# FFN hidden tiles in parts of 4, 4, 4, 4, 4, 2 in place of 4, 4, 4, 4, 6, with other look-ahead numbers

## Chip, core and metric

One NeuronCore of a Trainium2 chip runs the whole kernel as one launch. The metric is the device time of one execution in microseconds, the median of several runs.

## What is computed

A residual block on 512 tokens of width 1024 in float32: a SwiGLU FFN, a mixer stage (an HGRN2 recurrence and a Mamba-2 scan, merged by gates), a second SwiGLU FFN, a gated addition of per-layer embeddings, and a final RMSNorm. The change concerns the two FFNs only:

```python
D_MODEL, SEQ, D_FF = 1024, 512, 2816

def swiglu(x, w13, w2):
    gate, up = jnp.split(x @ w13, 2, axis=-1)
    return (jax.nn.silu(gate) * up) @ w2

h = h + 0.5 * swiglu(rms_norm(h, ffn1_norm[l]), ffn1_w13[l], ffn1_w2[l])
...                                        # mixer
h = h + 0.5 * swiglu(rms_norm(h, ffn2_norm[l]), ffn2_w13[l], ffn2_w2[l])
ple_gate = jax.nn.sigmoid(rms_norm(h, ple_norm[l]) @ w_ple_gate[l])
```

## The kernel before

**Numbers as pairs.** Every matmul operand is split into a high and a low part (`split`, L529 to L531: a cast on ScalarE, ACT, at L530 and a subtraction on VectorE, DVE, at L531). One product is three matmuls on TensorE, PE (`mm`, L518, L519, L520).

**The FFN.** The 2816 hidden columns are 22 tiles of 128, cut into the parts of `PARTS` (`ffn`, from L708). Hidden tiles are made two at a time (`gate_up`). Except for the first two tiles of all, a pair's gate and up columns are made by Strassen-Winograd: seven products instead of eight (`Seven`), each of 24 matmuls of 256 columns, one unit of the program each. Their weights come as one chunk of kind "w": five plain loads of 512 KB on the SP queue, two more that the POOL queue adds onto loaded pieces (L482), two sums on DVE (L503, L506), and seven pieces that are split.

**The down projection.** A part of four tiles keeps its hidden values in a `HiddenQ`: when its last pair is done (`put`), DVE makes four sums (`tsum`, L525, L527) and seven operands are split, 512 columns each. `down(k)` then is again seven Strassen products, one unit each, of 12 matmuls of 512 columns, with a "w" chunk of `w2` like that of `gate_up`. Each product is added to the tokens by two DVE operations (L780), 14 per part. The last part is another matter: its tiles lie in a `Hidden` (four splits of 256 columns per pair of tiles), and the function `last` does the plain product row by row: for each of the four token tiles t and two halves of the output, three matmuls of 512 columns per hidden tile, then one addition (L755). With six tiles these are 4 x 2 x 6 x 3 = 144 matmuls. Their weights are 6 chunks, one load and one split each.

**The order.** Units are emitted in a list. Part k's gate and up units stand merged with the down units of part k-1, after two units of their own:

```python
if k:
    U += x[:2] + _merge(x[2:], down(k - 1))
```

After the last part stand `n_end` (frees the normed input) and four units of `last`. Each ends with `done(t)`, which starts the norm of token tile t for the next stage (`norm_gen`, L565 to L569: a square on ACT, L567, two small POOL operations, a DVE multiplication, L569, then eight transposes on PE, L552, and four splits). After the first FFN the next units are the mixer's z projection, which takes one token tile after the other; after the second it is the gate projection of the embeddings. The list only fixes priorities and memory: a scheduler in the compiler orders each engine's instructions by its own simulated times, so work of later units can run ahead where it is ready.

**Look-ahead.** Before each unit, `run` (L443) loads and splits the pieces of later units, and loads raw ones further on. The six numbers of `AHEAD_FFN` are: how far ahead to split (near and far) and to load, in steps of 512 values per partition, and how many empty blocks of 4 KB per partition must be left by the near, far and raw ones (`room`). A piece of FFN weights counts 2 steps. All memory is one arena of 50 blocks; a load onto a block waits until the block's last reader is done.

Of the kernel before, what the change touches and what calls it, by code (L numbers as in the profile page):

```python
# [39 lines left out]
AHEAD = (4, 8, 10, 4, 8, 8)  # L40
AHEAD_SSD = (4, 9, 12, 4, 6, 8)
AHEAD_GATES = (2, 6, 8, 4, 8, 8)
AHEAD_FFN = (6, 10, 16, 1, 3, 3)

AGE = 130
PACK, PACK_MIX, PACK_GATES = 4, 2.5, 3
# [5 lines left out]

GATES_FIRST, LATE = 12, 2

PARTS = (4, 4, 4, 4, 6)

_INS = (
    "x", "p", "ffn1_norm", "ffn1_w13", "ffn1_w2", "mix_norm", "w_in", "conv_w", "conv_b", "dt_bias",
# [5 lines left out]
def _cols(c):  # L64
    return slice(c * P, (c + 1) * P)
# [281 lines left out]
class Block:  # L347
# [359 lines left out]
    def ffn(self, h, n, w13, w2, done, then=None):  # L707

        U = self.units
        start = len(U)  # L710
        f0s = [sum(PARTS[:k]) for k in range(len(PARTS) + 1)]
        N = len(PARTS)
        hid = [HiddenQ(self) for _ in PARTS[:-1]] + [Hidden(self, PARTS[-1])]
        v = self.nc.vector
# [19 lines left out]
        def gate_up(k, i):  # L734
            f = f0s[k] + i
            if f == 0:
                ch = [Chunk(w13, 0, KD, off, 2 * P, "c") for off in (0, FF)]
                return [Unit([c.halves[j] for j in range(2) for c in ch], first)]
            ch = Chunk(w13, 0, KD, f * P, 4 * P, "w", FF + f * P)
            q = Seven(self, n, lambda o, A, put=hid[k].put: gated(o, A, put, i))  # L740
            return [Unit([next(x for x in ch.halves if x.j == PRODUCTS[p][0])], lambda wt, p=p: q.product(wt, p, FFN_PACE))
                    for p in ORDER]
# [10 lines left out]
        def add(bank, t, ds):  # L753
            hd = h[0][t][:, ds * 512:ds * 512 + 512]
            v.scalar_tensor_tensor(hd, bank, 0.5, hd, ALU.mult, ALU.add)  # L755
            self.frb(bank)
# [30 lines left out]
        def last(*wt, t):  # L787

            q = len(wt) // 2
            for ds in range(2):  # L790
                bank = self.bank()
                for x in range(PARTS[-1]):
                    wh, wl = wt[ds * q + x // 2]
                    self.mm(bank, hid[-1].at(x, _cols(t)), (wh[:, x % 2], wl[:, x % 2]), x == 0, x == PARTS[-1] - 1)
                add(bank, t, ds)
# [13 lines left out]

        for k, size in enumerate(PARTS):  # L810
            x = [u for i in range(0, size, 2) for u in gate_up(k, i)]
# [9 lines left out]
        for u in U[start:]:  # L821
            u.ahead = AHEAD_FFN

# [808 lines left out]
```

## Time and profile before

| | us |
|---|---|
| median of 3 runs | 1578.18 (1575.81 to 1579.27) |
| the profiled execution | 1577.02 |
| its span in the trace | 1575.3 |
| PE busy in the span | 1537.3 |
| DVE busy in the span | 1081.1 |

The profiled execution has 1.7 us outside its span, and lies 1.2 us below the median. The first FFN fills the span from about 47 to 378 us, the second from about 1177 to 1523 us; the mixer lies between, the embedding gate behind. Matmuls overlap in the records (one of 512 columns is shown with 0.4 us, though they start 0.22 us apart), so a matmul's price is read from how many fit into a stretch without idle time.

### The profile page before, as it was taken

How to read it: one execution, taken by the hardware profiler on the slowest of the kernel's cores; microseconds unless marked ns; L12 is line 12 of the kernel's file. 1: busy time of each engine (PE TensorE's matmuls, PEld its weight loads, DVE VectorE, ACT ScalarE, POOL GpSimd, SP SyncE). 2: the span in 40 equal slices, each digit the busy share in tenths (PEclk: the TensorE clock that was granted, in tenths of full speed). 3: DMA queues.
4: the chain of work that ended last, by engine and by line, in shares of the span. 5: the costliest groups of instructions: out<-in, count | busy, mean ns of one | idle time of the engine just before them, and what ended most of it. 6: DMA issues, size and time to landing. Idle time of an engine off the chain costs nothing.

```text
span 1575.3 us, 22345 instructions
## 1 busy us (share of the span) xinstructions
PE 1537.3 (98%) x8894; PEld 1339.3 (85%) x8894; DVE 1081.1 (69%) x1379; ACT 754.5 (48%) x1093; POOL 173.3 (11%) x230
## 2 busy tenths in 40 slices
PE   8999999999998999999999999999999999999997
PEld 7989999988886887878888788888889999999986
DVE  7789888775568675867646654434348987897853
ACT  6555554554456445452454455433136654545542
POOL 2101101000012010110012011100002011001000
PEclk9999999999999999999999999999999999999999
DMA  9967867565233254364431522342239768676521
GB/s 298 213 160 189 214 147 192 123 208 161 67 95 108 88 167 141 120 182 141 121 100 61 174 69 72 107 134 94 94 90 236 171 175 206 148 193 148 200 68 54
DMA packets 216012, 225.52 MB, mean 143 GB/s; under 512 B 8148, under 2 KB 171748, under 8 KB 215908
## 3 DMA queue, kind: packets, MB, share of 16 engines
q1 hardware_dynamic: 190436, 194.73, 39.9%
q0 software_dynamic: 25472, 29.36, 11.7%
q8 instruction: 70, 1.15, 0.3%
q14 instruction: 34, 0.28, 0.0%
HBM read 209.31 MB, written 14.75 MB: 142 GB/s over the span
## 4 chain that ended last, share of the span: by engine, by line
PE 45%; DMA 5%; DVE 3%; ACT 2%; issue 1%; POOL 1%; DVEq 0%; POOLq 0%; ACTq 0%
PE bank L518 14%; PE bank L519 14%; PE bank L520 14%; DMA blk<-in_ffn_w_dram 4%; DVE blk L531 2%; ACT blk L530 1%; DMA blk<-in_w_in_dram 1%; PE bank L1336 0%; PE bank L1363 0%; PE bank L1331 0%; PE bank L1333 0%; PE bank L1351 0%; PE bank L1110 0%; PE bank L552 0%; PE bank L1365 0%
## 5 line engine op out<-in xcount | busy, mean ns | idle before, releaser
L518 PE MATMUL bank<-blk,blk 128*128 128x512 f32 (+1 forms) x2616 | 900.8, 346 | 17.4 <-ACT blk L530 7.7
L519 PE MATMUL bank<-blk,blk 128*128 128x512 f32 (+1 forms) x2616 | 898.2, 344 | 0.2 <-DVE blk L531 0.2
L520 PE MATMUL bank<-blk,blk 128*128 128x512 f32 (+1 forms) x2616 | 894.0, 344 | 2.5 <-DVE blk L531 2.5
L531 DVE TENSOR_TENSOR blk<-blk,blk 128x1024 fp32r<-128x1024 f32 (+2 forms) x477 | 493.7, 1059 | 206.0 <-ACT blk L530 166.4
L530 ACT CAST blk<-blk 128x1024 fp32r<-128x1024 f32 (+2 forms) x477 | 422.4, 920 | 388.2 <-DMA blk<-in_w_in_dram 79.2
L518 PEld LDWEIGHTS bank<-blk,blk 128*128 128x128 f32 x2616 | 498.0, 191 | 74.6 <-ACT blk L530 9.4
L520 PEld LDWEIGHTS bank<-blk,blk 128*128 128x128 f32 x2616 | 497.1, 191 | 56.0 <-DVE blk L531 2.9
L519 PEld LDWEIGHTS bank<-blk,blk 128*128 128x128 f32 x2616 | 498.8, 191 | 52.9 <-issue 1.0
L482 POOL DMA_DIRECT2D blk<-in_ffn_w_dram x56 | 70.8, 1265 | 484.0 <-DMA blk<-in_ffn_w_dram 384.6
L561 POOL TENSOR_SCALAR small<-small 128x1 f32<-128x1 f32 (+1 forms) x40 | 13.4, 334 | 615.2 <-ACT blk L567 293.6
L780 DVE SCALAR_TENSOR_TENSOR blk<-bank,blk 128x512 f32<-128x512 f32 x112 | 74.7, 682 | 2.3 <-PE bank L520 2.2
L883 ACT COPY blk<-bank 128x512 f32<-128x512 f32 x80 | 46.2, 581 | 45.5 <-PE bank L520 45.4
L995 DVE SCALAR_TENSOR_TENSOR blk<-bank,small,blk 128x511 f32<-128x511 f32 (+2 forms) x72 | 53.6, 744 | 15.1 <-ACT blk L993 14.4
L503 DVE TENSOR_TENSOR blk<-blk,blk 128x1024 f32<-128x1024 f32 x28 | 34.2, 1220 | 37.7 <-DMA blk<-in_ffn_w_dram 37.7
L748 ACT ACTIVATE blk<-blk 128x512 f32<-128x512 f32 x40 | 25.3, 632 | 61.7 <-DVE blk L893 45.8
L1110 PEld LDWEIGHTS bank<-blk,blk 128*128 128x128 f32 x256 | 40.9, 192 | 11.5 <-issue 6.0
L531 DVE TENSOR_TENSOR blk<-bank,blk 128x256 fp32r<-128x256 f32 x68 | 27.0, 418 | 18.8 <-ACT blk L530 18.7
L1110 PE MATMUL bank<-blk,blk 128*128 128x64 f32 x256 | 37.2, 259 | 1.6 <-DVE blk L531 1.6
L993 ACT ACTIVATE blk<-bank,small 128x512 f32<-128x512 f32 x24 | 18.6, 775 | 37.7 <-PE bank L520 37.7
L530 ACT CAST blk<-bank 128x256 fp32r<-128x256 f32 x68 | 23.4, 373 | 25.3 <-PE bank L552 25.1
L1071 DVE TENSOR_TENSOR blk<-blk,blk 128x1024 f32<-128x1024 f32 x16 | 19.6, 1222 | 21.6 <-POOL blk L1069 21.6
L506 DVE TENSOR_TENSOR blk<-blk,blk 128x1024 f32<-128x1024 f32 x28 | 34.1, 1216 | 0.0
(206 smaller groups left out, 1021.0 us busy)
## 6 DMA issues: line engine op xcount, KB each, us to landing
blk<-in_ffn_w_dram SPq DMA_DIRECT2D x160, 512.0 KB, 5.3
blk<-in_w_in_dram SPq DMA_DIRECT2D x89, 512.0 KB, 4.1
blk<-in_ffn_w_dram POOLq DMA_DIRECT2D x56, 512.0 KB, 8.4
blk<-in_w_ssm_out_dram SPq DMA_DIRECT2D x16, 512.0 KB, 4.0
blk<-cscr SPq DMA_DIRECT2D x16, 512.0 KB, 3.9
accscr<-blk SPq DMA_DIRECT2D x32, 256.0 KB, 2.4
blk<-accscr SPq DMA_DIRECT2D x32, 256.0 KB, 2.7
blk<-in_w_hg_out_dram SPq DMA_DIRECT2D x8, 512.0 KB, 4.5
```

The costliest lines, as they stand in the source:

```text
L482: self.nc.gpsimd.dma_start(c.raw[x], s, accum_op=ALU.add)
L503: v.tensor_tensor(raw["S2"], raw["S1"], raw["S2"], ALU.add)
L506: v.tensor_tensor(raw["S4"], raw["S2"], raw["S4"], ALU.add)
L518: t.matmul(out, lhsT=lh, rhs=rh, start=start, stop=False, skip_group_check=more)
L519: t.matmul(out, lhsT=lh, rhs=rl, start=False, stop=False, skip_group_check=more)
L520: t.matmul(out, lhsT=ll, rhs=rh, start=False, stop=stop, skip_group_check=more)
L530: self.nc.scalar.copy(hi, src)
L531: self.nc.vector.tensor_tensor(lo, src, hi.bitcast(F32), ALU.subtract)
L780: v.scalar_tensor_tensor(hd, bank, -0.5 if ds else 0.5, hd, ALU.mult, ALU.add)
L883: b.nc.scalar.copy(st[p], bank)
L995: nc.vector.scalar_tensor_tensor(t[:, s:], pc[:, 0:T - s], b.cw[:, 3 - s, ct:ct + 1], t[:, s:], ALU.mult, ALU.add)
L1110: nc.tensor.matmul(pyv[:, hh, :], lhsT=R[c][:, hh, :], rhs=xdt[:, hh, :], start=True, stop=True)
```

## The change

`PARTS` gets a fifth part of four tiles, with `HiddenQ` and `down`, and the last part, for `last`, keeps two tiles. The look-ahead of the FFN units gets other numbers: near 5 for 6, far 9 for 10, raw 14 for 16; blocks left empty 4, 6, 6 for 1, 3, 3.

```diff
-AHEAD_FFN = (6, 10, 16, 1, 3, 3)
+AHEAD_FFN = (5, 9, 14, 4, 6, 6)
...
-PARTS = (4, 4, 4, 4, 6)
+PARTS = (4, 4, 4, 4, 4, 2)
```

## Rows read from the trace of the kernel before

**Rows 1.** The page, part 1: busy us, share of the span, instructions.
```profile
PE 1537.3 (98%) x8894; PEld 1339.3 (85%) x8894; DVE 1081.1 (69%) x1379; ACT 754.5 (48%) x1093; POOL 173.3 (11%) x230
```
**Rows 2.** Windows, 25 us: length, busy PE, PEld, DVE, ACT, POOL (counts), clock, DMA share, GB/s.
```profile
50.00:75.00 25.00, 25.00 (x210) 25.00 (x210) 18.93 (x24) 14.80 (x19) 3.65 (x3) 1.00 0.79 198
1050.00:1075.00 25.00, 25.00 (x112) 20.68 (x112) 8.00 (x9) 7.71 (x10) 0.00 (x0) 1.00 0.34 111
```
**Rows 3.** Windows by stage, FFN 1 (part of four, part of six, `last`), FFN 2 (part of six).
```profile
149.00:208.00 59.00, 59.00 (x418) 55.55 (x418) 54.69 (x65) 33.14 (x42) 6.23 (x5) 1.00 0.72 177
267.00:345.00 78.00, 77.85 (x552) 73.25 (x552) 64.06 (x79) 44.30 (x61) 5.13 (x4) 1.00 0.64 171
345.00:378.00 33.00, 33.00 (x159) 27.27 (x158) 20.39 (x29) 14.49 (x27) 2.96 (x8) 1.00 0.60 179
...
1411.00:1490.00 79.00, 76.53 (x551) 72.19 (x550) 62.46 (x76) 44.41 (x61) 5.18 (x4) 1.00 0.64 180
```
**Rows 4.** Groups of instructions by form: count, busy us, mean ns, idle before.
```profile
L531 DVE TENSOR_TENSOR blk<-blk,blk 128x1024 fp32r<-128x1024 f32 x345 | 416.4, 1221 | 195.1 <-ACT blk L530 157.1 <-PE bank L519 24.0 <-PE bank L520 11.0
L530 ACT CAST blk<-blk 128x1024 fp32r<-128x1024 f32 x345 | 354.7, 1049 | 310.7 <-DMA blk<-in_w_in_dram 79.2 <-PE bank L519 64.5 <-DMA blk<-in_ffn_w_dram 47.0
...
L780 DVE SCALAR_TENSOR_TENSOR blk<-bank,blk 128x512 f32<-128x512 f32 x112 | 74.7, 682 | 2.3 <-PE bank L520 2.2
L531 DVE TENSOR_TENSOR blk<-blk,blk 128x512 fp32r<-128x512 f32 x108 | 72.1, 683 | 10.9 <-ACT blk L530 9.3 <-PE bank L519 1.5
...
L503 DVE TENSOR_TENSOR blk<-blk,blk 128x1024 f32<-128x1024 f32 x28 | 34.2, 1220 | 37.7 <-DMA blk<-in_ffn_w_dram 37.7
```
**Rows 5.** Windows of 25 and 2 us around the end of the first part, FFN 1.
```profile
75.00:100.00 25.00, 22.07 (x150) 20.52 (x149) 20.51 (x26) 11.84 (x18) 1.28 (x1) 0.93 0.53 133
...
90.00:92.00 2.00, 2.00 (x11) 2.00 (x11) 2.00 (x4) 0.36 (x1) 0.00 (x0) 0.50 0.00 0
```
**Rows 6.** Windows of 3 us at the ends of later parts of four.
```profile
263.00:266.00 3.00, 2.46 (x14) 1.94 (x13) 2.81 (x5) 2.70 (x5) 0.00 (x0) 1.00 0.09 19
...
1352.00:1355.00 3.00, 2.27 (x18) 2.03 (x17) 3.00 (x5) 3.00 (x4) 0.00 (x0) 1.00 0.00 0
1412.00:1415.00 3.00, 1.61 (x11) 1.29 (x10) 2.97 (x4) 2.46 (x4) 0.00 (x0) 1.00 0.15 39
```
**Rows 7.** Timeline (start, us, engine, line): end of the last gate product, both FFNs.
```profile
338.63 0.69 DVE L749 SCALAR_TENSOR_TENSOR blk<-bank,blk 128x512 f32<-128x512 f32 x1 [0.35 <-PE bank L520]
...
1486.63 0.28 PE L520 MATMUL bank<-blk,blk 128*128 128x256 f32 x1
...
1492.32 0.68 DVE L749 SCALAR_TENSOR_TENSOR blk<-bank,blk 128x512 f32<-128x512 f32 x1
...
1493.52 1.42 DVE L531 TENSOR_TENSOR blk<-blk,blk 128x256 fp32r<-128x256 f32 x4
```
**Rows 8.** Timeline, FFN 1: next weights' casts, then a token tile's norm.
```profile
329.76 2.00 ACT L530 CAST blk<-blk 128x1024 fp32r<-128x1024 f32 x2 [0.65 <-DMA blk<-in_w_in_dram]
...
351.39 1.06 ACT L567 ACTIVATE blk<-blk 128x1024 f32<-128x1024 f32 x1 [2.34 <-DVE blk L755]
...
353.50 1.28 DVE L569 SCALAR_TENSOR_TENSOR blk<-blk,small,blk 128x1024 f32<-128x1024 f32 x1 [1.24 <-POOL small L562]
...
359.50 1.20 ACT L530 CAST blk<-bank 128x256 fp32r<-128x256 f32 x4 [2.93 <-PE bank L552]
361.38 1.07 DVE L531 TENSOR_TENSOR blk<-bank,blk 128x256 fp32r<-128x256 f32 x3
```
**Rows 9.** FFN weight loads: KB each, us to landing; then an SP queue row.
```profile
blk<-in_ffn_w_dram SPq DMA_DIRECT2D x160, 512.0 KB, 5.3
...
blk<-in_ffn_w_dram POOLq DMA_DIRECT2D x56, 512.0 KB, 8.4
...
62.11 36.46 SPq L489 DMA_DIRECT2D blk<-in_ffn_w_dram  x8
```

## Prediction

> **What bounds the kernel.** I read the busy shares first, then windows by stage, then what PE waited for. PE is busy for 1537 of 1575 us [rows 1]: almost every saved microsecond of PE counts, and almost every new wait of PE costs in full. The windows show how close the next engine is: in a part of four tiles PE has no idle time, and DVE works 54.7 of 59 us, 93%; in the part of six, where one down projection is spread over three pairs of tiles, it is 64.1 of 78 us, 82%; in `last` 20.4 of 33 us, 62% [rows 3]. So the end of each FFN is now the stretch where DVE recovers, and that is the stretch which the change fills.
>
> **PE's price.** 210 matmuls of 256 columns fill 25 us, 0.119 us each; 112 of 512 columns fill 25 us, 0.223 us each [rows 2]. Part of six plus `last` now: 504 x 0.119 + (84 + 144) x 0.223 = 110.8 us, as the windows have it (78 + 33 = 111 us [rows 3]). After: a part of four (336 of 256 columns, 84 of 512), the part of two with the fifth down projection (168 and 84), and `last` with 48: 504 x 0.119 + (84 + 84 + 48) x 0.223 = 108.1 us. That is 84 + 48 = 132 matmuls in place of 144: 12 fewer per FFN, 2.7 us; in both, **-5.4 us**. Gate and up products are the same in number. `last` has no idle PE time [rows 3], so I take the full 0.223 us.
>
> The Trainium skill ("Perfetto Trace Analysis", Identifying the Most-Contended Engine) warns that matmul busy time overstates how full PE is and that LDWEIGHTS busy share is the better gauge. By it `last` is 27.3 / 33 = 83% full [rows 3], and the saving would be nearer 4.5 us. The rows disagree in what matters here: the count of matmuls that fit into a gapless window is the price of one, whatever the weight loads do, so I keep 5.4.
>
> **What DVE, ACT and the queues get.** Per FFN DVE gets 14 additions into the tokens (0.682 us each, 9.5 us); a "w" chunk's 7 splits and 2 sums (7 x 1.221 + 2 x 1.220 = 11.0) for 4 of the 6 plain splits that go (4.9); and in `put` 7 splits and 4 sums of 512 columns (11 x 0.68 = 7.5) for eight splits of half that width (2.7 if they cost half, 5.5 if as much) [rows 4]. Together +18 to +20 us. ACT gets 3 casts of 1.05 us [rows 4] and about as many small ones less or more. DMA gets 3 transfers of 512 KB more; 2 of the 7 new ones go through POOL's queue, where landing takes 8.4 us against 5.3 on SP's [rows 9]. POOL has nothing else to do there, so nothing stands behind its wait; behind an SP load that waits for its block stand all later loads.
>
> Where does this DVE work lie? The fifth part of four will look like the others: 93% DVE and still no PE idle time [rows 3]. The part of two has 38.7 us of PE, and DVE work of two "w" chunks (22.0), three takes and two gate multiplications (3.4), a small put (4 half splits, 1.4 to 2.7) and 14 additions (9.5): 36 to 38 us, 93 to 97% by the summed durations. By this PE still wins, without slack. I cost this work at nothing under PE's cover, except in three places.
>
> **A new boundary.** At the end of each part of four comes the burst of `put`, and ACT's casts delay the copies that free PE's banks. There are eight such boundaries now. Three later ones cost PE 0.54, 0.73 and 1.39 us [rows 6], four nothing; the first, where no down projection covers it, 2.9 us idle and, with the clock granted at 0.93 over 25 us, 1.75 us more [rows 5]. The change adds one covered boundary per FFN: mean of the seven covered 0.38 us, bounds 0 and 1.4. **+0.8 us** for both, 0 to 2.8.
>
> **The end of the last gate product.** Now the hidden values of the last two tiles are not urgent: 96 of the 144 matmuls of `last` use earlier tiles, 21 us of cover. In FFN 2 PE ended the product near 1486.8 and DVE read it only at 1492.3, with the splits ready at 1494.9; in FFN 1 DVE read it within 0.3 us [rows 7]. After the change all 48 matmuls need these two tiles. The only cover is the last down product, which the merge puts behind the last gate product: 12 x 0.223 = 2.7 us. The chain itself is 1494.94 - 1492.32 = 2.6 us and some 0.3 us until it starts: stall 0.2 us. If it starts as late as in FFN 2, 5.5 + 2.6 - 2.7 = 5.4 us. I take the FFN 1 row, since that delay is one the scheduler could afford: 0.25 each, **+0.5 us**, 0.4 to 10.8.
>
> **Norm into the next stage.** A token tile's norm is ready for the transposes 3.4 us after its tokens (351.39 to 354.78), then some 3 us of transposes and splits [rows 8]: 6.4 us, plus the first units' additions, 7. Before, three more token tiles (24 us) covered that of the first tile; after it is 36 x 0.223 = 8.0 us, just enough. The later tiles are needed 5.4 us of projection apart and come 2.7 us apart. I take **+0.5 us** for both FFNs; if DVE is late, see the second rival.
>
> **Look-ahead.** FFN pieces count 2 steps each, so near 6 and 5 both reach three pieces, far 10 and 9 both five: these two numbers do nothing. Raw loads reach 7 pieces instead of 8, and three more blocks must stay empty before a piece is taken. That keeps about one piece fewer in flight, one unit (24 x 0.119 = 2.9 us) of lead. SP's loads wait for blocks and not for their place in the list (eight loads took 36 us to issue [rows 9]), so an empty block also lets a load start earlier. No row shows which wins; from -4.7 (the stall of the first boundary goes, idle time and clock [rows 5]) to +4.7 per FFN (one more like it). The row nearest is the steady stretch, where a lead of one unit more or less meets no idle time [rows 3]: I take 0.
>
> **Sum.** -5.4 + 0.8 + 0.5 + 0.5 = -3.6 us. Against the profiled execution 1577.0 - 3.6 = 1573.4; the median of the runs lies 1.2 us above it, so the forecast for a median is 1578.2 - 3.6 = **1574.6 us**, with its own range 1573 to 1577.
>
> **Rivals.**
> - *Early read lost.* In one FFN the last gate product is read late, behind splits that wait for a DMA, as in FFN 2 now: -3.6 - 0.25 + 5.4 = +1.5 us, 1579.7. For it: the order on DVE is fixed by simulated times, and next-stage loads were late there. Against: FFN 1.
> - *DVE becomes the bound of the short tail, and the kernel gets slower.* From the last gate product to the first use of the norm PE has 60 matmuls and 16 transposes, 13.4 + 1.8 = 15.2 us. DVE must do in it two gate multiplications (1.4), four half splits (1.4), four additions of the last down products (2.7), eight of `last` (5.5), two norms (2.6) and four splits (1.4): 15.0 us. That is even, provided that the four weight pieces of the next stage are split before. Now they are, 9 us before the product ends [rows 8]. It decides by whether they still are: if not, 4 x 1.22 = 4.9 us per FFN come on top: -3.6 - 0.5 + 9.8 = +5.7 us, 1583.9.
> - *Weights arrive late.* The smaller look-ahead brings one more stall like the first boundary's in each FFN, 4.7 us with the clock at its lower level (1.2 GHz, 0.50 granted [rows 5]): -3.6 + 9.4 = +5.8 us, 1584.0. Against: PE waited for FFN weights hardly at all in the steady parts.
> - *The first boundary clears.* More empty blocks let the second part's loads start before it: -3.6 - 4.7 = -8.3 us, 1569.9.
> - That the change doesn't do what it says holds only for two of the look-ahead numbers, above.
>
> **How the numbers follow.** Chances: forecast 0.42 (0.30 of it below -3.2 us), first boundary clears 0.14, early read lost 0.16, DVE-bound tail 0.14, late weights 0.14 (of the last two 0.06 in one FFN only, near zero). 0.2% is 3.2 us, about what a measurement of this kernel can tell from no change. Faster: 0.30 + 0.14 = 0.44; within: 0.12 + 0.16 + 0.06 = 0.34; slower: 0.28 - 0.06 = 0.22. The range 1568 to 1585 leaves out more than one of the stalls at once, some 0.15.
>
> **What would show it.** Right: 24 PE matmuls fewer on each of L518 to L520 together, 140 L780 additions instead of 112, 60 accumulating loads instead of 56, `last` some 11 us long, PE idle time in each FFN up by about 1 us. Wrong: PE idle for more than 2 us before the first addition of `last` (early read), between `last` and the next projection (tail, with DVE without gaps there), or within the parts with the clock below 1 (late weights); the 75 to 100 us stretch without idle time (first boundary cleared). A difference of more than 4 us inside the mixer, whose code isn't touched, would also break the sum.

## The result, and the profile after

| | before | after |
|---|---|---|
| median of the runs, us | 1577.59 | 1615.66 (1613.54 to 1618.25) |
| ratio to before | 1 | 1.023, 95% interval 1.0208 to 1.0252 |
| span of the profiled execution, us | 1575.3 | 1612.7 |

The change makes the kernel 38 us slower, 2.3%; the forecast was 3.6 us faster. The counts came out as they were foretold: the page of the changed kernel (busy us, share, instructions) has 24 PE instructions fewer than [rows 1], and its groups have 140 additions and 60 accumulating loads.

```profile
PE 1547.0 (96%) x8870; PEld 1343.5 (83%) x8870; DVE 1116.7 (69%) x1423; ACT 762.5 (47%) x1097; POOL 179.8 (11%) x234
...
L482 POOL DMA_DIRECT2D blk<-in_ffn_w_dram x60 | 75.7, 1276 | 523.8 <-DMA blk<-in_ffn_w_dram 300.3
L780 DVE SCALAR_TENSOR_TENSOR blk<-bank,blk 128x512 f32<-128x512 f32 x140 | 93.6, 684 | 1.8 <-PE bank L520 1.8
```

So the work is what it was said to be, and PE's share of the span fell from 98 to 96%: PE has 27.7 us more idle time (65.7 for 38.0) and is busy 9.7 us longer with less work, since it ran at its lower clock after waits. What PE waited for (us in all, times, longest), first in the kernel before, then in the changed one:

```profile
PE bank L518 <- ACT blk L530: 7.7, 6, 2.2
PE bank L518 <- ACT blk L883: 3.9, 5, 1.4
...
PE bank L518 <- ACT blk L883: 18.7, 11, 3.6
PE bank L518 <- ACT blk L530: 14.0, 7, 4.0
PE bank L552 <- DVE blk L569: 6.4, 5, 3.0
PE bank L518 <- DVE blk L531: 5.6, 3, 5.2
```

L883 is the ACT copy that frees a bank of a gate product, L530 the cast of an operand, L569 the multiplication of the norm.

Where the 37.4 us of the two spans lie can be read from marks that both programs have: the second gate multiplication (L749, bank) of each pair of tiles, the first z activation (L912), the first output addition of the mixer (L1530), the first sigmoid of the embedding gate (L1594).

| stretch, us | before | after | difference |
|---|---|---|---|
| start to the end of the fourth part, FFN 1 | 261.8 | 270.9 | +9.1 |
| from there to the first z activation | 118.9 | 133.4 | +14.5 |
| mixer, to its first output addition | 713.1 | 712.7 | -0.4 |
| from there to the end of the fourth part, FFN 2 | 316.8 | 318.8 | +2.0 |
| from there to the first sigmoid | 117.3 | 129.6 | +12.3 |

The untouched mixer keeps its time. In both FFNs most is lost behind the fourth part, the stretch whose parts changed, where 2.7 us of PE work are gone; 11 us are lost in the first four parts, whose work is the same; there only the look-ahead numbers differ.

The short windows of the changed kernel (length, busy PE, PEld, DVE, ACT, POOL, clock, DMA share, GB/s) show the pattern: first four parts, FFN 1; fifth part and its boundary; end of FFN 1.

```profile
68.00:71.00 3.00, 1.40 (x5) 1.11 (x6) 2.02 (x2) 3.00 (x5) 0.00 (x0) 0.64 1.12 293
71.00:74.00 3.00, 3.00 (x16) 3.00 (x16) 0.43 (x1) 0.35 (x1) 0.00 (x0) 0.50 1.04 249
101.00:104.00 3.00, 1.22 (x10) 0.90 (x8) 0.70 (x1) 0.65 (x1) 0.01 (x1) 1.00 1.23 215
...
290.00:293.00 3.00, 0.73 (x4) 0.27 (x2) 1.23 (x1) 0.82 (x1) 0.00 (x0) 1.00 1.23 195
293.00:296.00 3.00, 2.23 (x11) 2.23 (x12) 2.74 (x3) 3.00 (x5) 0.00 (x0) 0.68 0.61 97
338.00:341.00 3.00, 0.02 (x1) 0.00 (x0) 3.00 (x5) 2.13 (x4) 0.00 (x0) 1.00 0.00 0
341.00:344.00 3.00, 2.42 (x12) 2.42 (x13) 3.00 (x5) 3.00 (x6) 0.00 (x0) 0.65 0.01 3
...
386.00:389.00 3.00, 0.74 (x7) 0.74 (x8) 2.55 (x4) 2.06 (x5) 2.64 (x4) 1.00 0.46 186
392.00:395.00 3.00, 2.84 (x10) 2.34 (x11) 3.00 (x8) 1.49 (x4) 0.00 (x0) 0.50 0.08 9
```

In these windows there are two kinds. At 101 and 290 us PE idles while DMA is full and DVE has little to do: weights are late. At 338 and 386 us DMA is nearly or half idle and DVE is busy without or nearly without a gap: the burst at a boundary, or the short end. Behind these waits, 2.7 to 3.6 us long, the granted clock falls to 0.50 (1.2 GHz) for a few us: they cost more than their own length. The Trainium skill ("TensorE: Matmul & The Clock Gate", Part 1: The HAM clock gate) has the same two levels, 1.2 and 2.4 GHz, and lets the clock follow how busy PE has been; the trace agrees.

What a late weight does is seen at 250 to 294 us of the changed kernel (what SP's queue waited for from 250 to 300 us; then timelines of POOL, DVE and ACT: start, us, engine, line, idle before and its releaser):

```profile
SPq L489 <- DVE blk L531: 27.1, 4, 20.9
...
282.94 1.28 POOL L482 DMA_DIRECT2D blk<-in_ffn_w_dram  x1 [18.00 <-DVE blk L531]
284.44 1.28 POOL L482 DMA_DIRECT2D blk<-in_ffn_w_dram  x1 [0.21 <-issue]
285.92 1.28 POOL L482 DMA_DIRECT2D blk<-in_ffn_w_dram  x1 [0.20 <-issue]
...
290.87 1.23 DVE L503 TENSOR_TENSOR blk<-blk,blk 128x1024 f32<-128x1024 f32 x1 [5.65 <-DMA blk<-in_ffn_w_dram]
...
292.18 1.04 ACT L530 CAST blk<-blk 128x1024 fp32r<-128x1024 f32 x1 [9.96 <-DVE blk L503]
293.13 0.58 ACT L883 COPY blk<-bank 128x512 f32<-128x512 f32 x1
```

SP issued no load for 20.9 us, up to 276.55 us, when a split on DVE ended and let the next load go. The plain loads onto which POOL's three loads add were issued behind that wait and landed at 282.4, 283.9 and 285.4 us; POOL issued each of its loads 0.56 us after that. So the 18.00 us before the first of them are not a queue on POOL, and the DVE split that the view names there, which ended 0.5 us after the landing, is not what it waited for. DVE's sum then waited for DMA, ACT's cast for DVE's sum, and behind the cast, in ACT's order, stood the copy L883 that frees PE's bank; PE idled 3.0 us for it. Before has waits of SP of this kind too, up to 17.7 us in the first FFN.

### The profile page after: what moved, and what is told of

The parts are those of the page before. It is cut to its first block, busy times and chain, and to the rows that moved or that the text cites. A ratio compares the mean times of both kernels' runs of the same rounds, so it can differ in the third digit from the quotient of the medians.

```text
span 1612.7 us, 22347 instructions
## 1 busy us (share of the span) xinstructions
PE 1547.0 (96%) x8870; PEld 1343.5 (83%) x8870; DVE 1116.7 (69%) x1423; ACT 762.5 (47%) x1097; POOL 179.8 (11%) x234
## 4 chain that ended last, share of the span: by engine, by line
PE 44%; DVE 5%; DMA 4%; issue 1%; ACT 1%; POOL 0%; DVEq 0%; POOLq 0%; ACTq 0%; SPq 0%
PE bank L518 13%; PE bank L519 13%; PE bank L520 13%; DMA blk<-in_ffn_w_dram 3%; DVE blk L531 2%; ACT blk L530 1%; DVE blk L780 1%; PE bank L1336 0%; PE bank L1363 0%; PE bank L1331 0%; DMA blk<-in_w_in_dram 0%; PE bank L1333 0%; DVE blk L503 0%; PE bank L1351 0%; DMA blk<-in_w_ple_gate_dram 0%
## 5 line engine op out<-in xcount | busy, mean ns | idle before, releaser
L518 PE MATMUL bank<-blk,blk 128*128 128x512 f32 (+1 forms) x2608 | 903.5, 348 | 40.0 <-ACT blk L883 18.7
L519 PE MATMUL bank<-blk,blk 128*128 128x512 f32 (+1 forms) x2608 | 898.0, 345 | 0.4 <-DVE blk L531 0.2
L530 ACT CAST blk<-blk 128x1024 fp32r<-128x1024 f32 (+2 forms) x481 | 430.8, 930 | 454.1 <-DMA blk<-in_ffn_w_dram 93.4
L531 DVE TENSOR_TENSOR blk<-blk,blk 128x1024 fp32r<-128x1024 f32 (+2 forms) x481 | 502.8, 1071 | 188.1 <-ACT blk L530 151.9
L518 PEld LDWEIGHTS bank<-blk,blk 128*128 128x128 f32 x2608 | 500.5, 192 | 101.5 <-ACT blk L883 22.6
L519 PEld LDWEIGHTS bank<-blk,blk 128*128 128x128 f32 x2608 | 500.9, 192 | 52.2 <-DVE blk L531 1.0
L482 POOL DMA_DIRECT2D blk<-in_ffn_w_dram x60 | 75.7, 1276 | 523.8 <-DMA blk<-in_ffn_w_dram 300.3
L780 DVE SCALAR_TENSOR_TENSOR blk<-bank,blk 128x512 f32<-128x512 f32 x140 | 93.6, 684 | 1.8 <-PE bank L520 1.8
L503 DVE TENSOR_TENSOR blk<-blk,blk 128x1024 f32<-128x1024 f32 x30 | 36.6, 1222 | 64.5 <-DMA blk<-in_ffn_w_dram 64.5
L883 ACT COPY blk<-bank 128x512 f32<-128x512 f32 x80 | 46.2, 582 | 34.0 <-PE bank L520 27.2
L531 DVE TENSOR_TENSOR blk<-bank,blk 128x256 fp32r<-128x256 f32 x68 | 26.5, 419 | 20.7 <-ACT blk L530 20.6
L552 PE MATMUL bank<-small,blk 128*128 128x128 f32 x136 | 28.1, 305 | 10.2 <-DVE blk L569 6.4
L506 DVE TENSOR_TENSOR blk<-blk,blk 128x1024 f32<-128x1024 f32 x30 | 36.6, 1218 | 0.1
L530 ACT CAST blk<-bank 128x256 fp32r<-128x256 f32 x68 | 23.9, 373 | 24.1 <-PE bank L552 23.5
L1071 DVE TENSOR_TENSOR blk<-blk,blk 128x1024 f32<-128x1024 f32 x16 | 21.3, 1336 | 19.2 <-POOL blk L1069 19.1
```

Of the source, the lines that this page charges most:

```text
L482: self.nc.gpsimd.dma_start(c.raw[x], s, accum_op=ALU.add)
L503: v.tensor_tensor(raw["S2"], raw["S1"], raw["S2"], ALU.add)
L506: v.tensor_tensor(raw["S4"], raw["S2"], raw["S4"], ALU.add)
L518: t.matmul(out, lhsT=lh, rhs=rh, start=start, stop=False, skip_group_check=more)
L519: t.matmul(out, lhsT=lh, rhs=rl, start=False, stop=False, skip_group_check=more)
L530: self.nc.scalar.copy(hi, src)
```

## Experiments

### Look-ahead alone, parts alone

e1 keeps the parts of before and takes the look-ahead numbers of after; e3 takes only the numbers of empty blocks, e4 only the reaches.

```diff
-AHEAD_FFN = (6, 10, 16, 1, 3, 3)
+AHEAD_FFN = (5, 9, 14, 4, 6, 6)      # e1
+AHEAD_FFN = (6, 10, 16, 4, 6, 6)     # e3
+AHEAD_FFN = (5, 9, 14, 1, 3, 3)      # e4
```

> The parts of before (4, 4, 4, 4, 6) with the look-ahead numbers of after (5, 9, 14, 4, 6, 6). Theory L (the smaller look-ahead makes weights late): in the changed kernel the fourth part ends 9.1 us later than before in the first FFN and 2.0 us later in the second, on the same work; so at least +11 us here, and with the part of six and the end under the same numbers +15 to +30 us. Theory P (the new parts cost the time, look-ahead is worth nothing): within 3 us of before.

Measured: 1583.9 us against 1577.3, ratio 1.0036 (1.0017 to 1.0056). Between the theories: the look-ahead numbers cost some 6 us, not 15 to 30. By the marks the first FFN loses 8.7 us up to the z activation, as far as the fourth part 9.8 us, so its part of six and `last` lose nothing; the second loses 4.0 us up to its fourth part and 1.0 us behind it.

> The parts of before, only the numbers of blocks left empty of after: (6, 10, 16, 4, 6, 6). Theory L1 (the empty blocks make the loss of look-ahead): nearly all of what the look-ahead numbers alone cost, +12 to +30 us. Theory L2 (the raw reach of 14 in place of 16 makes it): within 4 us of before.

Measured: 1583.2 us, ratio 1.004 (1.0026 to 1.0055), the same as e1, and outside both theories. With the blocks of after, the reach makes no difference to the total.

> The parts and empty blocks of before, only the reaches of after: (5, 9, 14, 1, 3, 3), of which 5 and 9 give the same program as 6 and 10. Theory L1: within 4 us of before. Theory L2: +10 us or more.

Measured: 1600.8 us, ratio 1.016 (1.0125 to 1.0195). One raw piece fewer costs 24 us with few empty blocks, and 0.7 us with many (e1 against e3). This fits L2, but e3's 6 us fit neither theory: the two numbers don't add. Fewer empty blocks beside a reach of 14 are worse than more.

e2 takes the parts of after, with the old numbers up to the end of the fourth part. Behind it the old numbers can't stand: a block would be asked for when none is left. That is why the change had to touch them; f3 below has the old reaches throughout, so only the empty blocks had to change.

```diff
 PARTS = (4, 4, 4, 4, 4, 2)
-AHEAD_FFN = (5, 9, 14, 4, 6, 6)
+AHEAD_FFN = (6, 10, 16, 1, 3, 3)
+AHEAD_TAIL = (5, 9, 14, 4, 6, 6)
...
-            u.ahead = AHEAD_FFN
+            u.ahead = AHEAD_FFN if i < tail else AHEAD_TAIL   # tail: first unit of the fifth part
```

> The parts of after (4, 4, 4, 4, 4, 2), with the look-ahead numbers of before for the units of the first four parts and those of after from the fifth part on (with the old numbers there too the arena runs out of blocks while the program is built). Theory L: the 11 us lost in the first four parts come back, some +27 us against before remain, all of them behind the end of the fourth part, where the numbers are still the small ones. Theory P: the same +27 us or more, since the new parts cause them; if L and P agree here, the stall table behind the fourth part decides: DVE waiting for FFN loads (L) or DVE busy without gaps (P). Theory M (the loss sits in the first four parts and is carried on): below +10 us.

Measured: 1595.6 us, ratio 1.0132 (1.0093 to 1.017): +18 us, between theory M's below 10 and the 27 of L and P. The fourth part ends at 260.9 us in place of 261.8 (FFN 2: 318.6 us from the mixer's mark, for 316.8), so the first four parts are as before within 2 us; behind it the stretch takes 126.8 and 125.9 us, +7.9 and +8.6, on 2.7 us less of PE work each. Windows of e2: from the last gate product to the next stage, in both FFNs.

```profile
356.00:387.00 31.00, 23.75 (x100) 17.94 (x100) 25.14 (x38) 16.75 (x31) 5.12 (x8) 0.89 0.61 196
...
1515.00:1546.00 31.00, 25.29 (x109) 19.68 (x108) 22.42 (x38) 11.86 (x27) 3.80 (x8) 0.89 0.21 74
```

In that stretch PE idles 7.3 and 5.7 us, and a clock of 0.89 over 31 us takes up to 3.4 us more (31 x 0.11; less where PE idles at the lower clock): up to 10.7 and 9.1 us. Before, the same stretches had no idle time and the full clock ([rows 3] for FFN 1). The new boundary, at the end of the fifth part, costs 0.9 and 0.7 us of idle time. The old one at the end of the fourth part got dearer in FFN 2: 4.0 us idle between 1417 and 1427 us, again with a lower clock behind it, where before loses 1.4 us [rows 6].

```profile
1420.00:1423.00 3.00, 0.00 (x0) 0.00 (x0) 2.83 (x5) 3.00 (x5) 0.00 (x0) 1.00 0.00 0
1423.00:1426.00 3.00, 2.70 (x16) 2.70 (x17) 3.00 (x5) 2.14 (x3) 0.00 (x0) 0.72 0.02 5
```

DVE and ACT are full there and DMA moves nothing: the burst of `put`, not late weights. PE waited 4.0 us for one L883 copy.

f3 asks which of the numbers makes the 20 us between e2 and after.

```diff
 PARTS = (4, 4, 4, 4, 4, 2)
-AHEAD_FFN = (5, 9, 14, 4, 6, 6)
+AHEAD_FFN = (6, 10, 16, 4, 6, 6)
```

> The parts of after with the reach of before and the empty blocks of after: (6, 10, 16, 4, 6, 6). With the parts of before the reach made no difference beside these blocks (e1 1583.9, e3 1583.2 us). Theory B (the empty blocks, which the new parts need so that the arena doesn't run out, cost the 20 us between e2 and after): 1610 to 1620 us. Theory R (the raw reach of 14 costs it): 1596 to 1604 us.

Measured: 1611.1 us, ratio 1.0212 (1.0176 to 1.0248). Theory B: the empty blocks, set from the first unit on, cost it. The total agrees with the changed kernel's, the places don't: against e2 f3 loses 2.8 us in the first four parts of FFN 1 and 7.3 us in those of FFN 2, the changed kernel 10.0 and 0.2 us.

### What is short at the end of each FFN

At the end of e2's first FFN (timelines of DVE and PE; L532, L750, L781 and L519 are before's L531, L749, L780 and L518), the splits of the next stage's weights, 1024 values wide, stand between the gate multiplications and the hidden tiles' own splits:

```profile
355.21 0.69 DVE L750 SCALAR_TENSOR_TENSOR blk<-blk,blk 128x512 f32<-128x512 f32 x1
355.81 1.22 DVE L532 TENSOR_TENSOR blk<-blk,blk 128x1024 fp32r<-128x1024 f32 x1
356.94 0.69 DVE L750 SCALAR_TENSOR_TENSOR blk<-bank,blk 128x512 f32<-128x512 f32 x1
357.55 0.76 DVE L532 TENSOR_TENSOR blk<-blk,blk 128x256 fp32r<-128x256 f32 x2
358.21 0.69 DVE L781 SCALAR_TENSOR_TENSOR blk<-bank,blk 128x512 f32<-128x512 f32 x1
358.81 1.22 DVE L532 TENSOR_TENSOR blk<-blk,blk 128x1024 fp32r<-128x1024 f32 x1
...
358.90 0.50 PE L519 MATMUL bank<-blk,blk 128*128 128x512 f32 x1 [1.54 <-ACT blk L531]
```

So DVE as the bound of the tail, the rival of the prediction, was tried first. f1 gives the low parts of six weight pieces per tail (two of `last`, four of the next stage) to POOL; g1 takes them off DVE without POOL, and leaves them out of the result.

```diff
             hf.pair = self.pair(*hf.raw.shape[1:])
-            self.split(hf.raw, *hf.pair)
+            if c.pool:                           # the six pieces of each tail
+                self.nc.scalar.copy(hf.pair[0], hf.raw)
+                self.nc.gpsimd.tensor_tensor(hf.pair[1], hf.raw, hf.pair[0].bitcast(F32), ALU.subtract)   # f1
+                self.nc.scalar.copy(hf.pair[1], hf.raw)                                                   # g1
+            else:
+                self.split(hf.raw, *hf.pair)
```

> The kernel of e2 (new parts, old look-ahead in the first four parts: 1595.6 us, +18 against before), with the low parts of the pieces that are split around each FFN's end (the two of the last rows and the first four of the next stage) made by POOL, which is idle there, and not by DVE: 6 subtractions of 1.22 us off DVE in each tail. In e2 DVE is busy without a gap from the last gate product into the rows of tokens, while PE idles. Theory D (DVE is the bound of the short tail): 4 to 8 us less per FFN, 1580 to 1588 us. Theory C (it is the chain behind the last gate product that nothing covers, wherever the subtractions are made): within 4 us of e2.

Measured: 1605.9 us, 10 us above e2, ratio 1.0172 (1.0139 to 1.0205). Outside both theories. The timeline of DVE and POOL in f1 shows why (L536, L785 and L901 are before's L531, L780 and L890; L499 is the subtraction on POOL):

```profile
340.11 1.21 DVE L536 TENSOR_TENSOR blk<-blk,blk 128x1024 fp32r<-128x1024 f32 x1
341.24 0.68 DVE L785 SCALAR_TENSOR_TENSOR blk<-bank,blk 128x512 f32<-128x512 f32 x1
341.85 2.83 DVE L536 TENSOR_TENSOR blk<-blk,blk 128x1024 fp32r<-128x1024 f32 x1
...
347.95 2.89 DVE L901 TENSOR_TENSOR blk<-blk,blk 128x512 f32<-128x512 f32 x1
...
340.26 16.16 POOL L499 TENSOR_TENSOR blk<-blk,blk 128x1024 fp32r<-128x1024 f32 x5 [24.27 <-DVE blk L785]
```

DVE's operations with both inputs in blocks that start while POOL subtracts take 2.8 us instead of 1.2 or 0.7; those that read a bank keep 0.68 us. f1 made DVE slower, so it is no test of the bound.

> The kernel of e2 (1595.6 us) with the same 6 subtractions per tail taken off DVE as in f1, but without POOL: ACT makes a second copy of the piece in place of the low part (the low parts of these weight pieces are left out of the result; ACT has 1.05 us more for each). In f1 the subtractions on POOL made DVE's own operations on two blocks 2.8 us long in place of 1.2, so f1 didn't test the bound. Theory D (DVE is the bound of the short tail): 4 to 8 us less per FFN, 1580 to 1588 us. Theory C (ACT's and DVE's order, with casts that wait for late weights ahead of the hidden tiles' splits, and the norm's own latency): within 4 us of e2, or above it, since ACT gets more.

Measured: 1595.0 us, ratio 1.0113 (1.0095 to 1.0131), where e2 has 1595.6. The total is theory C's: six operations less on DVE per tail, and no time gained beyond what the runs can tell apart. But it is no clean test of theory D either. ACT got the work that DVE lost; and five of the six second copies in FFN 1, all six in FFN 2, were done before PE ended the last gate product (358.2 and 1516.1 us). Behind it two wide splits still stood on DVE ahead of the hidden tiles' last split, where e2 has three.

f2 puts more cover behind the last gate product.

```diff
-                U += x[:2] + _merge(x[2:], down(k - 1))
+                d = down(k - 1)
+                cut = len(d) if k < N - 1 else 4
+                U += x[:2] + _merge(x[2:], d[:cut]) + d[cut:]
```

> The kernel of e2, but only four of the seven down products of the fifth part are merged into the gate units of the last pair; three stand behind the last gate product (8.0 us of PE work in place of 2.7). Theory C: the idle time behind the last gate product (2.7 and 3.7 us, and in the second FFN 3.4 us by the lower clock) goes, 6 to 10 us less than e2, 1586 to 1590 us. Theory D: DVE has the same work in the same time, the idle time moves to the norm behind: within 4 us of e2.

Measured: 1591.5 us, ratio 1.0084 (1.006 to 1.0109): 4 us below e2, less than theory C asked, more than D. In FFN 2 the stretch behind the fourth part shrinks from 125.9 to 120.4 us; in FFN 1 it is 128.3 for 126.8, with PE waiting in the rows of tokens and for the norm. Windows of f2, FFN 1:

```profile
352.00:355.00 3.00, 1.81 (x9) 1.17 (x8) 3.00 (x4) 1.46 (x2) 0.00 (x0) 1.00 0.50 144
364.00:367.00 3.00, 1.11 (x5) 0.66 (x4) 3.00 (x5) 0.65 (x1) 0.00 (x0) 1.00 1.03 311
370.00:373.00 3.00, 1.05 (x3) 0.33 (x1) 2.92 (x4) 2.60 (x6) 1.44 (x4) 0.75 0.22 89
```

h1 splits fewer weights ahead in the units of the last part; h2 adds f2 to it.

```diff
+AHEAD_END = (2, 4, 14, 4, 6, 6)
...
-            u.ahead = AHEAD_FFN if i < tail else AHEAD_TAIL
+            u.ahead = AHEAD_FFN if i < tail else AHEAD_TAIL if i < end else AHEAD_END   # end: first unit of the last part
```

> The kernel of e2 (1595.6 us), where the units of the last part (two tiles and the rows of tokens) split weights only one to two pieces ahead instead of three to five; the raw reach stays. In e2 splits of the next stage's weights, 1024 values wide, stand among the splits of the last hidden tiles on DVE, and casts that wait for late weights on ACT. Theory Q (these splits in ACT's and DVE's order hold up the last hidden tiles and the norm): the idle time behind the last gate product (2.7 and 3.7 us, with the lower clock some 7 us in the second FFN) shrinks, 4 to 10 us below e2. Theory N (the chains themselves are longer than the work that covers them): within 4 us of e2, or above it, since the next stage's weights are split later.

Measured: 1593.6 us, ratio 1.0101 (1.0073 to 1.0129), 2 us below e2: by the total, theory N. h1 did not clear DVE, though: two wide splits still stand behind the last gate product in either FFN.

> h1 and f2 together (f2, three down products behind the last gate product, was 1591.5 us). Theory Q: both gains, 1580 to 1587 us. Theory N: as f2, 1588 to 1595 us. Below before (1577) by neither, since the boundary of the fifth part and the norm's wait stay.

Measured: 1596.2 us, ratio 1.0111 (1.0078 to 1.0144): no second gain, and f2's isn't kept either. By the totals f2 takes away about a quarter of e2's 18 us, g1 and h1 hardly anything. The ends themselves say more (from PE's last gate product to the first activation of the next stage: length, PE's idle time, clock):

| | FFN 1, us | FFN 2, us |
|---|---|---|
| before (96 matmuls, 21.4 us, more) | 42.3, 0.0 idle, 1.00 | 41.1, 0.0 idle, 1.00 |
| e2 | 33.4, 7.3 idle, 0.90 | 31.4, 5.7 idle, 0.89 |
| g1 | 30.8, 5.2 idle, 0.94 | 29.2, 4.4 idle, 0.94 |
| h1 | 29.1, 5.5 idle, 1.00 | 28.5, 5.0 idle, 1.00 |
| f2 (24 matmuls, 5.4 us, more) | 40.0, 7.5 idle, 0.87 | 31.6, 2.9 idle, 1.00 |
| h2 (24 matmuls, 5.4 us, more) | 35.4, 5.0 idle, 0.95 | 32.5, 2.8 idle, 1.00 |

g1 and h1 shorten both ends by 2 to 4 us, and lose as much elsewhere. That is one profile each, and profiles differ by nearly as much on the same work: up to 326 us DVE and ACT run the same instructions in the same order in h1 and e2, yet the fourth part ends at 263.7 and 260.9 us. So the place of the wide splits may count for some us here, and no run cleared them away.

What is common to all is PE idling at the end of the FFN, behind chains that must run there one after the other: gate multiplication and splits of the only two tiles, rows of tokens, norm, transposes, splits. That these chains are what PE waits for is shown. Whether they are too long in themselves, or only by the weight splits in DVE's and ACT's order, stays open; no run lengthened the cover with work that needs nothing.

### More look-ahead on the kernel before

```diff
-AHEAD_FFN = (6, 10, 16, 1, 3, 3)
+AHEAD_FFN = (6, 10, 18, 1, 3, 3)      # f4
+AHEAD_FFN = (6, 10, 20, 1, 3, 3)      # g2
```

> The parts and empty blocks of before with a raw reach of 18 in place of 16: nine pieces, one more than before (e4, with seven, was 1600.8 us). Theory T (time falls steadily with the lead of the raw loads): 5 to 20 us below before. Theory S (the lead as such is enough at 16; what e4 lost comes from where the blocks and the accumulating loads happen to fall): anything from -5 to +25 us, with stalls at other places than before.

Measured: 1573.1 us, ratio 0.9971 (0.9952 to 0.999).

> The parts and empty blocks of before with a raw reach of 20, ten pieces. With 14, 16 and 18 the times were 1600.8, 1577 and 1573.1 us. Theory T (time falls with the raw lead until PE has no idle time left): at or below 1573 us. Theory S (where blocks and accumulating loads fall decides): anywhere from 1570 to 1600 us.

Measured: 1572.1 us, ratio 0.9971 (0.9958 to 0.9985). Both beat the kernel before and the changed one, by 5 us against before. With the old blocks the raw reach gives 1600.8, 1577, 1573.1 and 1572.1 us at 14, 16, 18 and 20. The order is theory T's, with most of the gain had at 16 and no difference between 18 and 20 that the runs can tell; but f4 falls just short of T's 5 us, and both times lie in theory S's range, so S isn't excluded. At a reach of 20 the first boundary [rows 5] has 1.1 us of idle time for 2.9, and the full clock (window of g2):

```profile
75.00:100.00 25.00, 23.88 (x168) 21.97 (x167) 24.47 (x31) 16.41 (x23) 2.56 (x2) 1.00 0.61 148
```

## Why the prediction was wrong

Two steps failed: the look-ahead at nothing, which cost 20 us, and the two stalls at the end of each FFN, given 1.0 us for both FFNs, which cost up to 10.7 and 9.1 us.

**PE's saving: the count is right, its price untested.** 24 matmuls are gone. That they are worth 5.4 us no run shows by itself, since PE was no longer what the end of the FFN waits for. The weighing against LDWEIGHTS' share didn't matter.

**DVE's added work at nothing: right in the parts.** DVE is busy 35.6 us longer (1116.7 for 1081.1), 17.8 us per FFN. In e2 PE has no idle time in the fifth part and the part of two outside the bursts behind the fourth and the fifth part. What DVE costs behind the last gate product comes below.

**The new boundary, 0.4 us each: right in e2, mis-sized in the changed kernel.** The end of the fifth part costs 0.9 and 0.7 us of idle time in e2, but 3.6 us with the lower clock behind it and 1.7 us in the changed kernel, where the bound was 1.4. The first boundary [rows 5], left out as uncovered, showed what a burst can cost, clock and all. That an old boundary gets dearer, as the fourth part's did in e2 (4.0 for 1.4 us), was no term of the sum.

**The end of the last gate product, 0.25 us each, and the norm, 0.25 us each: terms that failed.** Together they cost up to 10.7 and 9.1 us (e2). Both sums set one chain against one cover and found them equal (2.9 against 2.7, 7 against 8.0 us), and both took each instruction as starting at once.

The first sum chose FFN 1's row, where DVE reads the product within 0.3 us. In e2 it reads it 2.5 and 5.4 us after PE's end (354.4 and 1514.8 us), the delay of FFN 2's row [rows 7] that was taken as one the scheduler could afford, and three wide splits stand ahead of the hidden tiles' last split. PE waited 2.7 and 3.7 us. The second rival looked at this place, but asked only whether the next stage's first four pieces are split before. By the order of loads and casts they are in e2; the wide splits that stand here belong to pieces after them. Before, too, three wide splits stood behind the product, among these seven, but under 21 us of cover:

```profile
340.29 4.84 DVE L531 TENSOR_TENSOR blk<-blk,blk 128x1024 fp32r<-128x1024 f32 x7 [0.97 <-ACT blk L530]
```

The second sum gave the first token tile's norm the 36 matmuls of the other three as cover, 8.0 us. But PE didn't finish one token tile after the other. In e2 the first tile's two additions end at 366.7 and 1530.3 us, some 2.5 us before the last of the 48 matmuls ends, and the transposes wait 2.7 and 1.0 us for the norm, then again for later tiles (e2, FFN 1: the first four additions, the last matmul of `last`, the first transposes):

```profile
365.44 2.48 DVE L756 SCALAR_TENSOR_TENSOR blk<-bank,blk 128x512 f32<-128x512 f32 x4 [1.86 <-PE bank L521]
368.81 0.39 PE L521 MATMUL bank<-blk,blk 128*128 128x512 f32 x1
371.88 1.09 PE L553 MATMUL bank<-small,blk 128*128 128x128 f32 x8 [2.68 <-DVE blk L570]
```

**Look-ahead at 0: the step that failed most in kind.** The nearest row was said to be the steady stretch without idle time [rows 3]. That row shows that the look-ahead of before was enough, not that less would be. With the old parts the new numbers cost 6 us (e1), made by the empty blocks (e3). With the new parts they cost 20 us (after against e2, confirmed by f3). By the marks half of these 20 us is in the first four parts (270.9 for 260.9 us in the first FFN) and half behind them (133.4 for 126.8 and 129.6 for 125.9 us), although there the numbers are the same in both kernels. f3 has its losses in other places, so the total is shown, and where it falls is not. The rival "weights arrive late" named the mechanism, with DVE and ACT waiting for loads and PE for a copy behind them; it was given one such stall per FFN, and FFN 1 alone has two (101 and 290 us). That 5 and 9 change nothing was right: with them and with 6 and 10 the program is the same.

**The queues: right.** "Nothing stands behind its wait" holds for POOL: each of its 60 accumulating loads in the changed kernel was issued within 1.7 us of the landing of the plain load that it adds onto. The queue that held loads up was SP's, as the prediction said: 20.9 us behind one block.

**What stays open.** Why the stretch behind the fourth part needs 4 to 7 us more when the first four parts ran with more empty blocks; and why a raw reach of 14 is worse with few empty blocks (e4, 1600.8 us) than with many (e1, 1583.9 us). Both may depend on which block each load gets and who read it last; no run here took that apart.

**The range.** It allowed for one of the stalls at a time. The early read, the wide splits at the end and the late weights came together.

## What to carry over

A part made smaller to save matmuls also gives up the work that covered the next stage's chain: add up all chains that the remaining work must cover in that stretch, in their order, and ask for slack, not for equality. A memory limit that forces other numbers is part of the change's price: ask first whether the new layout fits with the old ones, and price the look-ahead by what the blocks allow, not by a stretch that never ran short. And try the opposite of a proposed cut: here a longer raw reach gave the 5 us that the cut in matmuls was to bring.

## What the runs showed of the hardware

DVE's operations with two block inputs that start while POOL runs a subtraction on two blocks take 2.8 us in place of 1.2 (1024 values) or 0.7 (512), and DVE's operations that read a bank are not held (0.68 us). The Trainium skill ("SBUF — State Buffer", Who interferes with whom) says that the two engines share a pair of ports, and that a DVE operation with two inputs in SBUF and a POOL operation that reads SBUF shut each other out, while one with a single such input doesn't; the trace agrees. Moving DVE work to an idle POOL made the kernel 10 us slower (f1 against e2), nearly all of it behind the fourth parts, where the subtractions are.

PE's clock made the waits dearer than they look: in e2 the stretch behind the last gate product lost 7.3 and 5.7 us to idle time, and up to 3.4 us each to the lower clock (0.89 over 31 us).
